# Storing the last 512 columns of the last half row in six transfers of 64, 15, 14, 13, 12 and 10 partitions

## The chip, the core and the metric

The kernel runs on one core of a Trainium2 chip. The core has compute engines that run side by side, each with its own instruction stream: TensorE (PE, unused here), VectorE (DVE), ScalarE (ACT), GpSimd (POOL) and SyncE (SP). Data moves between the chip's memory (HBM) and the on-chip memory (SBUF, 128 partitions) by transfers that an engine issues and that 16 transfer (DMA) engines carry out. Engines wait for each other and for transfers on semaphores.

The metric is the device time of one execution in microseconds (us), median of several runs. Before the change it is 932.68 us (three runs, 932.66 to 932.68). A profiled execution gives the trace; its "span" goes from the start of the program's first instruction to the end of its last one.

## What is computed

The input x is 8192 x 8192 in float32; the output is 8192 x 4096. It is a gated linear unit: the left half of each row times the sigmoid of its right half.

```python
def reference(x: np.ndarray) -> np.ndarray:
    a, b = np.split(x, 2, axis=-1)
    return a * (1 / (1 + np.exp(-b)))
```

The kernel reads 268.44 MB and writes 134.22 MB.

## The kernel before

**Tiles.** The rows go in 32 tiles of 256 rows: each of the 128 partitions holds two rows of x, one behind the other. A tile of x is 128 x 16384 numbers (64 KB in each partition), a tile of the output 128 x 8192 (32 KB in each). There are two input slots (`xs`) and two output slots (`os`), and tile i uses slot i % 2. Positions in a tile are counted in eighths: `(lo, hi)` in `store` are eighths of the output tile, so that `(6, 8)` is the last quarter of it, which is the second half of the second row of each partition, 2048 columns.

**One tile.** SyncE loads it (`load`, L63). ScalarE computes the sigmoid in place over the right halves (`work`, L82). GpSimd multiplies the first 3/16 of the columns and VectorE the rest (L84). ScalarE issues the store (`store`, L68). The first and the last tile are worked in four pieces of 2048 columns, all on VectorE. The first tile is loaded and stored in two halves; the last one is stored as `(0, 4)`, `(4, 6)` and `(6, 8)`, and `behind[-1] = 1` puts the store of a piece behind the sigmoid of the next piece on ScalarE.

**Order and waits.** The order on each engine is that of the program text (`place` keeps it). `place` also drops every wait but those named: a store waits for the multiplies of its piece, a load for the multiplies that last read its slot, the sigmoid for its load and, in the middle tiles, for the store that frees the output slot. The framework gives each transfer, of loads and stores alike, one of eight semaphores in turn. A transfer that takes a semaphore waits on its engine until the one that had it before is over, where the engine doesn't know that already.

**Start and end.** `_launch_early` moves the first load ahead of the start-up barrier. `_close_on_sync` rewrites the end of the program. It finds the semaphore `last` of the last transfer that ScalarE issues in program order (L137). GpSimd waits for the other engines' drains, then for every other transfer and engine (one event for each wait; two waits can share an instruction), drains, clears all semaphores but `last` and drains again; SyncE has one instruction, which waits for `last` and sets it back:

```python
last = [i for i in body if i.engine == ACT and i.opcode == "DMACopy"][-1].sync_info.on_update[0].id
...
    block[:] = [
        *arrive,
        drain1,
        gather1,
        *(event(POOL, w) for w in waits.sync_info.on_wait if w.id != last),
        reset,
        *clears,
        drain2,
        event(SP, final[0], [back]),
    ]
```

In the profile the events and drains of the end stand under L186 (`tc.compile()`), the clears under L152.

Of the kernel before, what the change touches and what calls it, by code (L numbers as in the profile page):

```python
# [8 lines left out]
def _tiles(ctx, tc, x, out):  # L9
    nc = tc.nc  # L10
    P = nc.NUM_PARTITIONS
    DEP = mybir.DependencyInfo(mybir.DependencyClass.Sync, mybir.DependencyReason.DATA)
    fp32 = mybir.dt.float32
    SIG = mybir.ActivationFunctionType.Sigmoid

    n_rows, n_cols = x.shape
    half = n_cols // 2
    R = 2
    SLOTS = 2
    n_tiles = n_rows // (P * R)  # L20
    x_g = x.rearrange("(g p h r) m -> g h p (r m)", p=P, h=2, r=R)
    out_g = out.rearrange("(g p h r) m -> g h p (r m)", p=P, h=2, r=R)

    pool = ctx.enter_context(tc.tile_pool(name="io", bufs=1))
    xs = [pool.tile([P, R * n_cols], fp32, name=f"x_sb{k}") for k in range(SLOTS)]
    os = [pool.tile([P, R * half], fp32, name=f"o_sb{k}") for k in range(SLOTS)]

    whole = [(0, 8)]
    rows = [(0, 4), (4, 8)]
    cut = half // 16 * 3  # L30
    few_and_most = [(0, 8, 0, cut), (0, 8, cut, half)]
    fourths = [(k, k + 2, k % 4 * half // 4, (k % 4 + 2) * half // 4) for k in range(0, 8, 2)]
    loads = [whole] * n_tiles
    works = [few_and_most] * n_tiles
    stores = [whole] * n_tiles
    behind = [0] * n_tiles
    loads[0] = stores[0] = rows
    works[0] = works[-1] = fourths
    stores[-1] = [(0, 4), (4, 6), (6, 8)]
    behind[-1] = 1  # L40

    def meet(a, b):
        return a[0] < b[1] and b[0] < a[1]

    traced = [[] for _ in range(SLOTS)]
    load_of, mul_of, store_of = {}, {}, {}

    def place(i, ins, *needs):


        kept = {n.ins.name for n in needs}
        for e in traced[i % SLOTS]:
            if e.ins.name not in kept:
                tc.declare_no_dep(ins.ins, e.ins, reason="follows from the waits that are kept")
        traced[i % SLOTS].append(ins)
        tc.keep_in_program_order(ins)
        return ins

    def load(i):
        for lo, hi in loads[i]:  # L60
            c = slice(lo * n_cols // 4, hi * n_cols // 4)
            free = [m for w, m in mul_of.get(i - SLOTS, []) if meet(w, (lo, hi))]
            ins = nc.sync.dma_start(out=xs[i % SLOTS][:, c], in_=x_g[i // 2, i % 2, :, c])  # L63
            load_of.setdefault(i, []).append(((lo, hi), place(i, ins, *free)))

    def store(i, lo, hi):
        c = slice(lo * half // 4, hi * half // 4)
        ins = nc.scalar.dma_start(out=out_g[i // 2, i % 2, :, c], in_=os[i % SLOTS][:, c])  # L68
        done = [m for w, m in mul_of[i] if meet(w, (lo, hi))]
        store_of.setdefault(i, []).append(((lo, hi), place(i, ins, *done)))  # L70

    def work(i, lo, hi, near, far):

        rows = xs[i % SLOTS].rearrange("p (r h m) -> p r h m", r=R, h=2)
        packed = os[i % SLOTS].rearrange("p (r m) -> p r m", r=R)
        r, c = slice(lo // 4, (hi + 3) // 4), slice(near, far)
        b = rows[:, r, 1, c]
        landed = [s for w, s in load_of[i] if meet(w, (lo, hi))]
        gone = [s for w, s in store_of.get(i - SLOTS, []) if meet(w, (lo, hi))]
        by_sigmoid = 0 < i < n_tiles - 1  # L80
        needs = [*landed, *(gone if by_sigmoid else ())]
        sig = place(i, nc.scalar.activation(out=b, in_=b, func=SIG), *needs)  # L82
        engine = nc.gpsimd if far == cut and i > 1 else nc.vector
        mul = engine.tensor_mul(out=packed[:, r, c], in0=rows[:, r, 0, c], in1=b)  # L84
        if by_sigmoid:
            for s in gone:
                tc.add_manual_dep(sig.ins, s.ins.name, DEP, reason="frees the output slot")
        place(i, mul, sig, *(() if by_sigmoid else gone))
        mul_of.setdefault(i, []).append(((lo, hi), mul))

    for i in range(SLOTS):
        load(i)
    for i in range(n_tiles):
        due = list(stores[i])
        for k, piece in enumerate(works[i]):
            work(i, *piece)
            ready = works[i][k - behind[i]][1] if k >= behind[i] else 0
            while len(stores[i]) > 1 and k < len(works[i]) - 1 and due[0][1] <= ready:
                store(i, *due.pop(0))
        if i + SLOTS < n_tiles:  # L100
            load(i + SLOTS)
        for lo, hi in due:
            store(i, lo, hi)
# [71 lines left out]
@with_exitstack  # L175
def kernel(
    ctx: ExitStack,
    tc: tile.TileContext,
    x: bass.AP,
    out: bass.AP,  # L180
):
    nc = tc.nc
    with ExitStack() as pools:
        _tiles(pools, tc, x, out)
    tc.close()
    tc.compile()  # L186
    _launch_early(nc)
    _close_on_sync(nc)
# [30 lines left out]
```

## Time and profile before

| what | value |
|---|---|
| median of 3 runs | 932.68 us |
| the profiled execution, its time | 932.5 us |
| its span | 931.1 us |
| read and written | 268.44 MB and 134.22 MB, 432 GB/s over the span |
| VectorE, ScalarE, GpSimd busy | 232.5, 229.8 and 99.9 us |
| last multiply ends (VectorE) | 922.75 us |
| last store is issued (ScalarE) | 922.78 us |
| GpSimd's last instruction ends | 929.32 us |
| SyncE's last instruction ends | 931.12 us |

The compute engines are busy for a quarter of the span or less. The profile's rows name a source line, an engine and an operation; "q" behind an engine (ACTq, POOLq) marks what its sequencer does, such as issuing a transfer or waiting on a semaphore. "us to landing" is the time from the issue of a transfer until its completion semaphore has its last increment. A transfer on 128 partitions gives sixteen such increments, one from each transfer engine, and the trace has the time of each.

### The profile page before, as it was taken

The numbers are of one execution on the slowest core, as the hardware profiler recorded it, in microseconds if no ns is written. First come the engines' busy times: TensorE is split into PE (matmuls) and PEld (weight loads), VectorE is DVE, ScalarE is ACT, GpSimd is POOL, SyncE is SP. The second block draws the span as 40 slices with busy tenths as digits, with TensorE's granted clock in tenths as the row PEclk, the third lists the DMA queues.
The fourth block names the chain that finished last, engine by engine and source line by source line (L and its number), as shares of the span: only waits on it lengthen the run. The fifth ranks groups of instructions, "written<-read, shape, count | busy, mean of one in ns | idle before, by whom it ended". The sixth has DMA issues, their size and how long they took to land.

```text
span 931.1 us, 325 instructions
## 1 busy us (share of the span) xinstructions
DVE 232.5 (25%) x39; ACT 229.8 (25%) x69; POOL 99.9 (11%) x33
## 2 busy tenths in 40 slices
DVE  1133311333113331133320333203332033320233
ACT  2123332033320333203332023320233302333023
POOL 0001111011110111101111011110111101111010
DMA  9999999999999999999999999999999999999998
GB/s 405 450 439 417 428 450 424 455 405 428 450 428 450 407 469 409 428 450 427 452 405 450 428 428 450 424 452 408 428 450 428 450 408 465 411 428 450 427 452 383
DMA packets 9793, 402.67 MB, mean 432 GB/s; under 512 B 1088, under 2 KB 1088, under 8 KB 1088
## 3 DMA queue, kind: packets, MB, share of 16 engines
q1 hardware_dynamic: 4752, 268.44, 66.6%
q10 hardware_dynamic: 5040, 134.22, 33.4%
q14 instruction: 1, 0.01, 0.0%
HBM read 268.44 MB, written 134.22 MB: 432 GB/s over the span
## 4 chain that ended last, share of the span: by engine, by line
DMA 75%; DVE 12%; ACT 12%; issue 0%; ACTq 0%; SPq 0%
DMA out_dram<-o_sb 65%; DVE o_sb L84 12%; ACT x_sb L82 12%; DMA x_sb<-in_x_dram 10%; ACTq L68 0%; SPq L63 0%
## 5 line engine op out<-in xcount | busy, mean ns | idle before, releaser
L84 DVE TENSOR_TENSOR o_sb<-x_sb 128x6656 f32<-128x6656 f32 (+2 forms) x39 | 232.5, 5970 | 690.2 <-ACT x_sb L82 690.2
L82 ACT ACTIVATE x_sb<-x_sb 128x1536 f32<-128x1536 f32 (+1 forms) x68 | 228.5, 3407 | 689.9 <-DMA out_dram<-o_sb 630.0
L84 POOL TENSOR_TENSOR o_sb<-x_sb 128x1536 f32<-128x1536 f32 x29 | 99.7, 3437 | 787.7 <-ACT x_sb L82 787.7
L82 ACT ACT_TABLE_LOAD x1 | 1.3, 1283 | 0.8 <-PEq L203 0.8
L203 POOL MEMSET const-float32-0.0<- 128x1 f32 x1 | 0.1, 98 | 0.2 <-issue 0.2
L203 POOL MEMSET const-bfloat16-1.0<- 128x1 bf16 x1 | 0.1, 101 | 0.0
L203 POOL MEMSET const-uint8-127<- 128x1 uint8 x1 | 0.1, 101 | 0.0
L203 POOL MEMSET const-float32-1.0<- 128x1 f32 x1 | 0.1, 98 | 0.0
## 6 DMA issues: line engine op xcount, KB each, us to landing
out_dram<-o_sb ACTq DMA_DIRECT2D x30, 4096.0 KB, 43.6
x_sb<-in_x_dram SPq DMA_DIRECT2D x2, 4096.0 KB, 16.4
out_dram<-o_sb ACTq DMA_DIRECT2D x3, 2048.0 KB, 28.0
out_dram<-o_sb ACTq DMA_DIRECT2D x2, 1024.0 KB, 8.3
x_sb<-in_x_dram SPq DMA_DIRECT2D x31, 43.5
```

Source lines behind the costliest of these rows:

```text
L82: sig = place(i, nc.scalar.activation(out=b, in_=b, func=SIG), *needs)
L84: mul = engine.tensor_mul(out=packed[:, r, c], in0=rows[:, r, 0, c], in1=b)
L203: nc = _bacc.Bacc("TRN2", target_bir_lowering=False, num_devices=1)
```

## The change

The last store of the last tile, 128 partitions x 2048 columns (8 KB in each partition), becomes seven transfers, issued one behind the other by ScalarE: first 1536 columns of all 128 partitions, then the last 512 columns (2 KB in each partition) of partitions 0 to 63, 64 to 78, 79 to 92, 93 to 105, 106 to 117 and 118 to 127. All of them wait for the same multiply as the one store did. Everything else is as before; the bytes written are the same.

With seven transfers in place of one, the last transfer in program order, whose semaphore is `last` in `_close_on_sync`, is that of partitions 118 to 127. Three of the new transfers wait for an older transfer that had their semaphore: the one of 14 partitions for the store of tile 29, that of 12 for the store of tile 30, that of 10 for the store `(0, 4)` of the last tile.

```diff
+    EDGE = 512
...
     def store(i, lo, hi):
-        c = slice(lo * half // 4, hi * half // 4)
-        ins = nc.scalar.dma_start(out=out_g[i // 2, i % 2, :, c], in_=os[i % SLOTS][:, c])
+        first, end = lo * half // 4, hi * half // 4
+        pieces = [(0, P, first, end)]
+        if (i, hi) == (n_tiles - 1, 8):
+            pieces, p = [(0, P, first, end - EDGE)], 0
+            for n in (64, 15, 14, 13, 12, 10):
+                pieces.append((p, p + n, end - EDGE, end))
+                p += n
+            assert p == P
         done = [m for w, m in mul_of[i] if meet(w, (lo, hi))]
-        store_of.setdefault(i, []).append(((lo, hi), place(i, ins, *done)))
+        for p, q, a, b in pieces:
+            ins = nc.scalar.dma_start(out=out_g[i // 2, i % 2, p:q, a:b], in_=os[i % SLOTS][p:q, a:b])
+            store_of.setdefault(i, []).append(((lo, hi), place(i, ins, *done)))
```

## The prediction, made before the result was known

> **What bounds the kernel now.** I read the page first, then the chain of waits from 897 us on, then the timeline of the last microseconds, and last the rows of the two source lines that close the program.
>
> ```profile
> GB/s 405 450 439 417 428 450 424 455 405 428 450 428 450 407 469 409 428 450 427 452 405 450 428 428 450 424 452 408 428 450 428 450 408 465 411 428 450 427 452 383
> HBM read 268.44 MB, written 134.22 MB: 432 GB/s over the span
> out_dram<-o_sb ACTq DMA_DIRECT2D x2, 1024.0 KB, 8.3
> ```
>
> Transfers run at one rate from the first slice to the last, so the bytes set the time, and the change moves none of them. It can only act on what follows the last multiply. The timeline there:
>
> ```profile
> 918.13 0.34 ACTq L68 DMA_DIRECT2D out_dram<-o_sb  x1
> 920.33 2.79 ACTq L68 DMA_DIRECT2D out_dram<-o_sb  x2
> 920.46 2.29 DVE L84 TENSOR_TENSOR o_sb<-x_sb 128x2048 f32<-128x2048 f32 x1 [0.16 <-ACT x_sb L82]
> ```
>
> The last multiply ends at 922.75 and the last store is issued at 922.78. That row of the page says a 1 MB store lands 8.3 us after its issue: 931.1, the end of the span. Those 8.3 us are a queue, not a latency: by the trace's landing records the last four stores landed at 921.34, 926.20 (2 MB), 928.64 and 931.09 (1 MB each), so 4.86 us for 2 MB and 2.44 for 1 MB. The transfer engines have work without a gap until the end, and an issue is early by several microseconds. Last, the closing instructions, on GpSimd and on SyncE:
>
> ```profile
> L186 POOLq EVENT_SEMAPHORE  x5: 17/43/5235, 923.3 to 928.9; - x5
> L186 POOLq DRAIN  x2: 34/58/83, 929.0 to 929.3; - x2
> L152 POOLq EVENT_SEMAPHORE_RANGE_CLEAR  x2: 66/68/69, 929.1 to 929.2; - x2
> L186 SPq EVENT_SEMAPHORE  x1: 17/17/17, 931.1 to 931.1; - x1
> ```
>
> GpSimd waits for every store but the last one: its wait of 5.235 us (from 923.44) ends at 928.67, 0.03 after the store before the last has landed. Four short waits, a drain, two clears and a drain follow, and it is done at 929.32: **0.68 us after that landing**. SyncE alone waits for the last store, and its one wait is over 0.03 after it. So GpSimd's closing lies beside the 2.44 us of the last store, with 1.8 us to spare.
>
> **The change part by part.** Sums are made against the profiled execution: span 931.1, time 932.5, which is 0.18 under the median of 932.68.
>
> *Issues.* One issue on ScalarE becomes seven. An issue row is 0.34 us with some 0.04 between, so 6 x 0.38 = 2.3 us more on ScalarE, from 923.12 to about 925.4. The semaphores of transfers are used again in turn, eight in all, so three of the new issues also wait for older transfers. The 14-row piece needs the store issued at 868.2 and the 12-row piece the store that landed at 921.34; both are over. The 10-row piece needs the 2 MB store, landed at 926.20, so it goes out at 926.2 to 926.6. Nothing is queued behind it on ScalarE but the drain, for which GpSimd's closing waits at its start, and the last bytes are due only near 930.5. Cost 0; the cover is the queue of bytes. From an issue to a first packet the first load shows about 1.0 us, so an issue could be about 2.5 us later before it costs. SyncE's queue is empty by then and GpSimd issues no transfer.
>
> *Bytes on each engine.* The two sizes give the price of a row. A store of 8 KB rows takes 2.44 us for 8 rows on each of the 16 engines, 0.306 a row; 16 KB rows take 4.86, 0.607. So 8 KB cost 0.3016 and a row itself about 0.004; a 6 KB row is 0.230 and a 2 KB row 0.080. A completion mark is 0.009 in the packet records. Before, each engine has 8 x 0.306. After, it has 8 x 0.230 = 1.84, four rows of the 64-row piece, and, if the five small pieces put one row each on an engine, none to five more. With nine small rows that is 1.84 + 0.72 + 0.05 for five or six more marks = 2.61, or **+0.17 us**; with four it is 2.17, or **-0.27 us**. The 16 marks of the last store land between 930.54 and 931.09: twelve within 930.70, then 930.80, 930.85, 930.90 and 931.09. If the latest engine gets four small rows, it ends at 930.82, and the ordinary ones, with nine, at up to 930.87. If it gets nine it ends at 931.26. The trace does not number its engines, so I take the middle, 931.07, and keep 930.87 and 931.26 as ends.
>
> [...]
>
> *The closing.* This is the step that costs. The last store by program order, for which SyncE waits, is now the 10-row piece. GpSimd waits for all the others, and the 1536-column store and five of the small pieces now end with the whole: no more than one 2 KB row (0.09) before it. The 1.8 us of cover are gone. The six others land at 930.82 to 931.17, in the middle 931.0; 0.68 more makes GpSimd's end 931.68 (ends 931.5 and 931.85), and that is the new end of the span: **+0.56 us** (+0.38 to +0.73).
>
> *Behind the span.* The profiled execution has 1.4 us there. The trace's semaphore records show one semaphore (number 2) counted up at 929.84 and 929.89, then at 931.26 and four more times to 931.42. The first is 0.52 after GpSimd's last instruction, 931.26 is 0.14 after SyncE's. I read this as the engines signing off in turn, SyncE last. If GpSimd is last, its own 0.52 and two steps of 0.05 and 0.04 follow it, 0.61 instead of 0.14: **+0.47 us**. The ends are 0 (the pairing is mine and no view names it) and 0.47; I take 0.47, as it is the nearest record.
>
> Sum: 0.56 + 0.47 = 1.03; 932.5 + 1.03 = 933.53 in the profiled execution, 933.7 for the median.
>
> **The rivals.** All against 0.2% (1.87 us: 930.81 and 934.55), about what a measurement of this kernel can tell from no change.
>
> *A, the closing stays hidden or the balance pays.* The late engine gets four small rows (-0.22), nothing is added behind the span, and the 10-row piece lands well after the others, since it is issued over 1 us after them. For it: late marks keep their offsets over the last ten stores (+0.44, +0.26, +0.21, +0.16), so they belong to fixed engines. Against it: with bytes queued until 930.5 the late issue changes no order. Time: 932.68 - 0.22 = 932.5, up to 932.8 if half of GpSimd's 0.68 shows.
>
> *B, neighbouring rows share a way out of memory.* Every transfer of this trace spans all 128 partitions, and 432 GB/s over 16 engines is what those give; a piece of 15 neighbouring rows has no row here. One end is 0. [...] As the pieces before the last end 0.22 earlier, 933.7 + 1.4 - 0.2 = 934.9; with two pieces overlapping, about 934.2. From 0.84 us on it makes the change slower by over 0.2%.
> [...] I take the nearest row, full rate, and keep this as the upper end.
>
> *C, the small pieces pile up (the other side: slower).* 15, 14, 13, 12 and 10 rows don't divide over 16 engines. If a piece lies on one engine or a few, one engine gets up to 64 rows at 0.080 instead of five: +4.7 us, 938.4. It decides from 16 rows on one engine: 11 more than five at 0.080 are 0.9 us. Against it: all records of 128-row stores show 16 marks, the rows shared out.
>
> **How the numbers follow.** The forecast (closing laid bare, rows at full rate, 932.9 to 934.3) has 0.62; A 0.15 (932.4 to 932.8); B 0.18 (933.9 to 935.0, some 0.07 of it above 934.55); C 0.05. No mechanism takes 1.87 us off: 0.01 for faster, from A. Slower is 0.07 + 0.05 = 0.12, the rest, 0.87, is within 0.2%. The range goes from A's 932.4 to B's 934.9.
>
> **What would show it.** GpSimd's last drain should end after SyncE's last wait, near 931.7, as the end of the span; its long wait should end near 931.0, not 928.67. ScalarE should show eight issues after 920 us, the last at 926.2. The last landing should be 930.9 to 931.3; 932 and later speaks for B, 934 and later for C. If GpSimd ends before SyncE, the step on the closing was wrong. If its end is last but the time behind the span stays at 1.4 us, the 0.47 was.

## The result and the profile after

The changed kernel takes **934.65 us** (median of 15 runs, 934.47 to 934.80) against 932.68 us before (15 runs, 932.60 to 933.04): +1.97 us, a ratio of 1.0021 with a 95% interval of 1.0013 to 1.0029. The forecast was 933.7 with a range to 934.9, so the direction and about half of the size were there. The interval is clear of 1, but it leaves open on which side of the forecast's mark of 0.2% the change lies. The profiled execution shown here has a time of 934.65 and a span of 932.8.

The bytes and their rate are the same. The lines of the page that answer to those of before, with the last store now in seven parts (of each row of issues: the number, the size of one transfer and its time from issue to landing, where the page has one):

```profile
HBM read 268.44 MB, written 134.22 MB: 432 GB/s over the span
out_dram<-o_sb ACTq DMA_DIRECT2D x1, 1024.0 KB, 8.3
out_dram<-o_sb ACTq DMA_DIRECT2D x1, 768.0 KB, 8.2
out_dram<-o_sb ACTq DMA_DIRECT2D x1, 128.0 KB, 8.1
out_dram<-o_sb ACTq DMA_DIRECT2D x1, 30.0 KB, 7.0
```

The wide part is a quarter smaller than the store that it came from, yet it lands 8.2 us after its issue instead of 8.3. By the forecast's prices of a row, 8 x 0.306 before and 8 x 0.230 now, it should have saved some 0.6 us. That is the first thing to explain.

The timeline of the last microseconds, and ScalarE's issue rows (duration in ns: least, median, most):

```profile
920.61 10.10 ACTq L78 DMA_DIRECT2D out_dram<-o_sb  x8
920.74 2.29 DVE L93 TENSOR_TENSOR o_sb<-x_sb 128x2048 f32<-128x2048 f32 x1 [0.16 <-ACT x_sb L91]
```
```profile
L78 ACTq DMA_DIRECT2D out_dram<-o_sb x7: 338/1221/1653, 923.1 to 930.4; - x7
```

Seven issues take from 923.06 to 930.70, not to 926.6. The first and the last take 0.34, those between take 0.98 to 1.65. That is the second thing to explain.

The closing, by its source lines (number of instructions, duration in ns, start of the first and the last):

```profile
L195 POOLq EVENT_SEMAPHORE  x5: 17/43/354, 931.0 to 932.4; - x5
L195 POOLq DRAIN  x2: 34/58/83, 932.4 to 932.7; - x2
L195 SPq EVENT_SEMAPHORE  x1: 17/17/17, 932.5 to 932.5; - x1
L161 POOLq EVENT_SEMAPHORE_RANGE_CLEAR  x2: 48/68/88, 932.5 to 932.6; - x2
```

SyncE's wait for the last store is over at 932.485; GpSimd still drains and clears until 932.775, and that is now the end of the span. Before it was the other way round, with 1.8 us between them.

The last mark of each transfer, from the trace's landing records, in us. I take these for the marks of one transfer engine, the latest: before the change the last mark of each of the last ten stores came 0.42 to 0.46 us behind the middle of its sixteen. One column is one transfer; the last row is the distance from the mark before:

```
                 1 MB     1536 columns   64     15     14     13     12     10
before  928.64   931.09
after   928.89   931.23                  931.57 931.75 931.93 932.10 932.28 932.45
step             2.35                    0.34   0.18   0.18   0.17   0.18   0.17
```

The execution after is 0.25 us behind from earlier on (928.89 against 928.64). Measured from there, the last mark came 2.44 us later before and 3.56 us later now: **the landing is 1.1 us later**. Two places hold it. The 1536 columns take 2.35 instead of the 1.84 that their rows cost, 0.5 too much; and the five small pieces take 0.176 each where a row and a mark were to cost 0.089.

Behind the span the order of the signing off shows as forecast: semaphore 2 goes up 0.52 after GpSimd's last instruction, at 933.30, then at 933.34 and 933.37. The time at which it reached SyncE's step was 931.26 before: 2.11 later, or 1.86 without the 0.25.

### The profile page after: what moved, and what is told of

Same layout as the page of the kernel before. It is cut to its first block, busy times and chain, and to the rows that moved or that the text cites. A ratio compares the mean times of both kernels' runs of the same rounds, so it can differ in the third digit from the quotient of the medians.

```text
span 932.8 us, 331 instructions
## 1 busy us (share of the span) xinstructions
DVE 232.5 (25%) x39; ACT 229.8 (25%) x69; POOL 99.8 (11%) x33
## 4 chain that ended last, share of the span: by engine, by line
DMA 75%; DVE 12%; ACT 12%; issue 0%; ACTq 0%; SPq 0%
DMA out_dram<-o_sb 65%; DVE o_sb L93 12%; ACT x_sb L91 12%; DMA x_sb<-in_x_dram 10%; ACTq L78 0%; SPq L64 0%
```

## The experiments

Three theories stood at the start, and the expectations add a fourth. **Closing**: 0.75 us of the loss is GpSimd's closing laid bare. **Sharing**: the rest comes from transfers of few or neighbouring partitions, which keep each other from the full rate. **Issues**: the rest comes from ScalarE's slow issues, which let the transfer engines run dry. **Price of a transfer**: each further one costs some 0.2 us, whatever its shape. All times below are medians of ten runs beside runs of the kernel before on the same chip (932.66, 932.61 and 932.64 us in the three groups), unless it is said that there was one. The 95% intervals of the ratios reach about 0.1% to each side, and those of e4 (0.9996 to 1.0015) and e5 (0.9998 to 1.0016) hold 1; there the single runs and the marks in the traces have to carry the reading.

### The closing alone

e1 is the kernel before with the two waits of the closing exchanged:

```diff
-    last = [i for i in body if i.engine == ACT and i.opcode == "DMACopy"][-1].sync_info.on_update[0].id
+    last = [i for i in body if i.engine == ACT and i.opcode == "DMACopy"][-2].sync_info.on_update[0].id
```

> The kernel before, with one store per piece as it was; only the closing is exchanged: SyncE waits for the store before the last, GpSimd for the last one. Theory 'closing laid bare': GpSimd is done 0.68 us after the last landing (931.1 + 0.7 = 931.8) and signs off 0.6 later, so +1.1 us: 933.8. Rival 'the closing is not on the path': 932.7.

Measured: 933.76, +1.10 us (ratio 1.0010, 1.0000 to 1.0019). No transfer has changed. The closing rows of e1:

```profile
L186 POOLq EVENT_SEMAPHORE  x5: 17/43/7671, 923.7 to 931.7; - x5
L186 POOLq DRAIN  x2: 34/58/83, 931.8 to 932.0; - x2
L186 SPq EVENT_SEMAPHORE  x1: 17/17/17, 929.0 to 929.0; - x1
```

GpSimd's long wait (from 923.78, 7.671 us) ends at 931.45 with the last landing, its last drain at 932.08; semaphore 2 goes up 0.52 after that. A closing that starts when the last transfer lands costs this kernel 1.1 us.

e2 is the changed kernel with the closing mended: SyncE waits for all seven transfers of the last store, and GpSimd neither waits for their semaphores nor clears them.

```diff
-    last = [i for i in body if i.engine == ACT and i.opcode == "DMACopy"][-1].sync_info.on_update[0].id
-    final = [w for w in waits.sync_info.on_wait if w.id == last]
+    copies = [i for i in body if i.engine in (ACT,) and i.opcode == "DMACopy"][-7:]
+    late = sorted({c.sync_info.on_update[0].id for c in copies})
+    final = [w for c in copies for w in waits.sync_info.on_wait if w.id == c.sync_info.on_update[0].id]
...
-        *(event(POOL, w) for w in waits.sync_info.on_wait if w.id != last),
+        *(event(POOL, w) for w in waits.sync_info.on_wait if w.id not in late),
...
-        event(SP, final[0], [back]),
+        *(event(SP, w, [b]) for w, b in zip(final, back)),
```

> The changed kernel, but SyncE waits for all seven transfers of the last store and GpSimd only for what is older, so that its clears lie beside the last transfers again. In the trace of the changed kernel SyncE's sign-off would come at 932.62 instead of 933.37, so theory 'the closing costs 0.75 of the loss' expects 933.9; the rest, 1.2 us, is the later landing. If the closing costs nothing: 934.65.

Measured: 933.85, 0.80 less than the changed kernel. Its closing rows:

```profile
L200 SPq EVENT_SEMAPHORE  x7: 17/17/17, 931.3 to 932.6; - x7
L200 POOLq DRAIN  x2: 34/58/83, 931.3 to 931.5; - x2
```

GpSimd is done at 931.55, while SyncE's seven waits follow the marks of the latest engine, from 931.34 to 932.58. So of the 1.97 us the closing holds 0.8, and 1.2 are the later landing. All the kernels below but e8 and e10 have the mended closing (for as many transfers as they have in the last store), so that they show the landing alone.

### Full and half transfers

e3 and e4 store the last 512 columns in one transfer of 128 partitions, and in two of 64:

```diff
-            pieces, p = [(0, P, first, end - EDGE)], 0
-            for n in (64, 15, 14, 13, 12, 10):
...
+            pieces = [(0, P, first, end - EDGE), (0, P, end - EDGE, end)]   # e3
+            for n in (64, 64):                                              # e4
```

> The last 512 columns in one transfer of all 128 partitions behind the one of 1536 columns, closing mended as in e2 (SyncE waits for both). Theory 'sharing' (only rows of neighbouring partitions without the other half cost): 932.7, one mark and eight short rows more, 0.05. Theory 'issues' (ScalarE's slow issues set the end): 932.7 too, one issue more is far from late. Theory 'price of a transfer' (every further transfer costs 0.2 or so whatever its shape): 932.9.

Measured: 932.70, +0.04: no difference. One more full transfer was as good as free here.

> The last 512 columns in two transfers of 64 partitions each, closing mended. [...] Theory 'issues': two issues of 1.3 us end by 926.2, nothing late: 932.7. Theory 'price of a transfer': 932.9 to 933.0.

Measured: 933.38, +0.72. Issues and price of a transfer had put it at 932.7 and at 933.0 at most. With a wide row held up by 0.5 as in the changed kernel (728 ns instead of 234) the 932.70 of e3 becomes 933.2, so of the theories sharing is left. e12 then changes only which partitions are in a half, the even and the odd ones instead of the lower and the upper:

```diff
+            pieces = [(0, P, first, end - EDGE)]
+            pieces += [(slice(k, P, 2), None, end - EDGE, end) for k in range(2)]
```

> As e4 (1536 columns, then two transfers of 64 partitions, closing mended), but the two take every second partition, the even and the odd ones, instead of the lower and the upper half. [...] If 64 rows in a transfer cost by themselves: 933.4 as e4.

Measured: 932.73, +0.09 us. The same number of transfers, rows and issues as e4, and the loss is gone: the ten runs of e4 took 933.17 to 933.49, those of e12 932.65 to 932.89. The transfers issued after the last multiply, in e4 and in e12 (size of one, time from issue to landing):

```profile
out_dram<-o_sb ACTq DMA_DIRECT2D x1, 768.0 KB, 8.3
out_dram<-o_sb ACTq DMA_DIRECT2D x2, 128.0 KB, 7.8
```
```profile
out_dram<-o_sb ACTq DMA_DIRECT2D x1, 768.0 KB, 7.7
out_dram<-o_sb ACTq DMA_DIRECT2D x2, 128.0 KB, 7.2
```

It is the wide transfer *ahead* of the half one that lands 0.6 us later in e4. The packet records say how: in e3 and e12 all 128 rows of 6 KB take 234 ns; in e4 one takes 791 ns, in the changed kernel one takes 728, in e2 764, in e6 638, in e7 720. In e2, e4, e6 and e7 the next longest 6 KB row takes at most 248 ns; in e11, below, four take 295 to 846. The latest engine is still at its last wide row when the others have begun with partitions 0 to 63 (in the changed kernel from 930.18 on, the first of the others at 929.76), and by these records that row goes at about a third of its rate (728 against 234). Rows of the half transfer suffer too: a 2 KB row takes up to 346 ns in e4 and never over 84 in e12. In e10, below, 64 partitions come directly behind the 1 MB store, and there it is an 8 KB row of that store that takes 747 ns instead of 309. So it is shown that the choice of partitions makes the loss, and with it the 0.5 us on the wide part. On which side the sharing lies is not: with the partitions the runs also changed which rows of the output in HBM are written at the same time. In this choice of partitions and of output rows alone e4 and e12 differ, by 0.65 us.

### The small pieces

e6 makes the small pieces even, four times 16 neighbouring partitions; e7 takes every fourth partition for each of the four instead.

```diff
+            for n in (64, 16, 16, 16, 16):                                                       # e6
...
+            pieces = [(0, P, first, end - EDGE), (0, 64, end - EDGE, end)]                       # e7
+            pieces += [(slice(64 + k, P, 4), None, end - EDGE, end) for k in range(4)]
```

> After the 1536 columns 64 partitions and then four times 16 neighbouring ones, closing mended: one row on each engine, even. Theory 'sharing': as e2 with four one-row pieces instead of five, at the 0.18 that their marks lie apart on the latest engine: 933.7. Theory 'uneven pieces' (a piece that doesn't fill 16 engines is what costs): 933.4, as e4, or less.

Measured: 933.62, 0.23 under e2, or 0.18 when each is taken against its own runs of the kernel before. Sixteen rows in each piece are no cure; one piece less saved about its 0.18.

> As e6, but each piece of 16 takes every fourth partition of 64 to 127 instead of 16 neighbours. [...] If the 0.18 is the price of a row with its mark whatever its partition, as e6: 933.7.

Measured: 933.64, as e6 (933.62): in the time the choice of the partitions makes no difference here. The marks of the latest engine are 0.18 apart in both (e6: 931.46, 931.64, 931.81, 931.99, 932.16; e7: 931.44, 931.62, 931.80, 931.97, 932.15). For the latest engine it did not matter which neighbours a piece has; in both runs 0.18 was the price of a transfer that puts one row on an engine.

In the packet records the neighbours did matter. From 930.8 on, when the last piece of 16 is under way, ten rows of 2 KB take 101 to 265 ns in e6; in e7 none takes over 88. In the changed kernel five rows at 931.2 take 113 to 161. But these rows lie on engines that are done before the latest one, whose small rows take 84 ns in both kernels, so the time does not show them.

e11, with one run, has pieces that halve:

```diff
-            for n in (64, 15, 14, 13, 12, 10):
+            for n in (64, 32, 16, 8, 4, 2, 2):
```

> After the 1536 columns pieces of 64, 32, 16, 8, 4, 2 and 2 partitions, closing mended. A look at the marks: the latest engine's mark should go on in steps of 0.18 as long as it takes part. [...] Time with sharing: 933.5 to 934.2.

Measured: 934.21, at the upper edge. The latest engine's marks come at 931.25 (the wide one), 931.60 (64), 931.78 (32), 931.96 (16), 932.13 (8), 932.31 (4), 932.48 (2) and 932.65 (2). Each transfer has one: the latest engine took part even in those of two rows. And 32 partitions, two rows on an engine, cost the same 0.18 as one row, while four rows cost 0.34. So two marks of this engine stood no closer than about 0.175, and two rows of 2 KB with their mark (2 x 0.080 + 0.009 = 0.17) just fill that time.

In the changed kernel the landing records of the transfers of 15, 14, 13, 12 and 10 partitions show as many marks, from 930.70 on, and one record more for each, 0.09 to 0.17 us after its issue ends (926.48, 927.58, 928.84, 930.50 and 930.88). The latest engine's mark is there in each, so it got nine small rows, not four.

### The issues

e5 cuts the last store into seven transfers of all 128 partitions, 288 or 296 columns each:

```diff
+            at = [first + n * (end - first) // 7 // 8 * 8 for n in range(7)] + [end]
+            pieces = [(0, P, a, b) for a, b in zip(at, at[1:])]
```

> The last store in seven transfers as in the changed kernel, but each of all 128 partitions (288 or 296 columns), closing mended. Theory 'sharing': nothing shares a way, so only rows and marks: 48 rows and 6 marks more on each engine at 0.004 and 0.009, some 0.25 us, 932.9. Theory 'issues': the issues are as slow as in the changed kernel (about 1.3 us each, the last one done near 930.7), each brings only 0.35 us of bytes, so the engines run dry and the last lands near 932: 933.7. Theory 'price of a transfer' (0.18 for each further one instead of 0.09): 933.2.

Measured: 933.28, +0.67. The issue rows of e5:

```profile
L75 ACTq DMA_DIRECT2D out_dram<-o_sb x7: 338/1184/1277, 923.1 to 929.3; - x7
```

Five of them are about as slow as in the changed kernel (the last two take 0.65 and 0.46), with no small and no uneven piece, so it is not the shape that makes an issue slow. But the marks of the latest engine come 0.42 to 0.44 us apart without a hole (929.39, 929.83, 930.26, 930.70, 931.13, 931.57, then 931.96), so the latest engine did not wait for the issues, and the 933.7 of that theory was missed. The time came out where "price of a transfer" had put it, yet the rows explain most of it: a row of 1152 or 1184 bytes takes 51 or 52 ns in the packet records, not 46. Seven transfers of eight such rows and a mark are 7 x (8 x 0.0515 + 0.009) = 2.95 us against 2.48 for the one store in the same records: 0.47 of the 0.54 by which the last mark came later. My row price, fitted to rows of 8 and 16 KB, was too low for short ones.

e9 has SyncE issue the six pieces:

```diff
-            ins = nc.scalar.dma_start(out=out_g[i // 2, i % 2, p:q, a:b], in_=os[i % SLOTS][p:q, a:b])
+            engine = nc.sync if b - a == EDGE else nc.scalar
+            ins = engine.dma_start(out=out_g[i // 2, i % 2, p:q, a:b], in_=os[i % SLOTS][p:q, a:b])
```

> The changed kernel with the closing mended as in e2, but SyncE issues the six pieces, in a queue of its own, while ScalarE issues the 1536 columns. Theory 'issues': SyncE's issues take 0.34 each, all out by 925.5, so the time falls to 932.9. Theory 'latest engine' (the held-up wide row and 0.18 for each piece on the latest engine): the same work is on that engine, only in another order: 933.3 to 933.9.

Measured: 934.14, above both expectations. The issue rows:

```profile
L79 SPq DMA_DIRECT2D out_dram<-o_sb x6: 547/1267/1619, 923.0 to 929.5; - x6
L79 ACTq DMA_DIRECT2D out_dram<-o_sb x1: 338/338/338, 923.0 to 923.0; - x1
```

SyncE's queue holds nothing older (its last load landed at 912.0), and its issues are as slow. The two queues also mix: the wide transfer lands at 931.76, 0.4 later than in e2, and 6 KB rows of up to 447 ns show that more of them are held up. An issue that is slow because of its own engine's queue is out.

e8, with one run, has the same pieces cut from the first store of the program:

```diff
-        if (i, hi) == (n_tiles - 1, 8):
+        if (i, hi) == (0, 4):
```

> A look at the issue rows: the same six pieces cut from the first store of the program, when ScalarE's queue holds nothing older; the closing is as before the change. Theory 'backlog' (an issue is held while ScalarE's older transfers are queued): 0.34 us each. Theory 'behind another' (an issue directly behind another one takes 1.0 to 1.6 whatever is queued): 1.0 to 1.6 again. Time 932.7 to 934.

```profile
L78 ACTq DMA_DIRECT2D out_dram<-o_sb x7: 292/387/823, 18.4 to 21.6; - x7
```

Neither theory: 0.29 to 0.82, with 0.53 and 0.82 for the second and the third and 0.29 to 0.39 for the others. So an issue directly behind another isn't slow by itself. What makes it slow at the end of the program was not settled. The time of e8, 935.17, points to a cause of its own: six more transfers shift the turn of the eight semaphores, and SyncE's load of tile 2 now has that of the load of tile 1, which is in flight until 45.7. The load of tile 2 lands at 72.90 instead of 70.46, and the span is 2.7 us longer; the delay was not tried by itself. The timelines from 18 us on, before and in e8:

```profile
28.15 0.33 SPq L63 DMA_DIRECT2D x_sb<-in_x_dram  x1
```
```profile
45.83 0.33 SPq L64 DMA_DIRECT2D x_sb<-in_x_dram  x1
```

e10 puts the six pieces ahead of the wide transfer, with the closing as the change left it:

```diff
             assert p == P
+            pieces = pieces[1:] + pieces[:1]
```

> The changed kernel with its own closing, but the six pieces are issued before the 1536 columns, so that the last transfer is a wide one of 1.84 us and covers GpSimd's 0.68 again. If the slow issues (1.0 to 1.6 each) put the wide store's issue near 930, the engines run dry before it and it lands near 933: 934.5 to 935. If they don't matter: the 0.75 of the closing is saved and the pieces cost their 0.62 or less: 933.0 to 933.8.

Measured: 933.36, where the second expectation put it, though not for its reason. The issue rows:

```profile
L79 ACTq DMA_DIRECT2D out_dram<-o_sb x7: 340/532/1655, 922.9 to 928.7; - x7
```

The last transfer is a wide one again, so GpSimd is done at 930.92, beside it. But its 16 marks lie within 0.24 us (931.75 to 931.99), where in the other kernels with a wide part at the end they are spread over 0.6 to 1.3: all engines began it together, that is, they had run dry and waited for its issue at 928.67. By the packet records 5 of the 16 engines were at work on the mean from 928.6 to 929.5. Here the slow issues do set the end, and the time stayed low because the last three issues were short again (0.39, 0.34 and 0.36). In the changed kernel the issues come close to setting the end, no more: from 930.6 to 931.6 some 5 of the 16 engines are at work, the others wait for pieces, but the latest one has its steps of 0.18 to the end.

## Why the prediction was right or wrong

Right, by its own steps:

- **The closing is laid bare.** GpSimd ends after SyncE and ends the span. e1 has it alone at +1.10, the sum of the forecast's 0.68 and 0.47 less the few hundredths that SyncE's own wait took; e2 finds 0.80 of it in the changed kernel. It is less there because GpSimd waits for the semaphores one after another: before, three more waits followed the one that ended with the landing; behind the landing of the 12-row piece (932.28) only one more does, so 0.50 instead of 0.68 followed. (The forecast counted four short waits behind the long one; its row has three, as the first of the five is the wait for the drains. The 0.68 was read from the ends and stands.)
- **The sign-off behind the span.** 0.52 after GpSimd's end and 0.07 to SyncE's step, as read from the semaphore records before.
- **Rivals A and C.** The closing did not stay hidden, the latest engine did not get four rows, and the 10-row piece landed 0.17 behind the piece before it, so A is out. Each small piece has as many marks as rows, so nothing piled up on one engine, and C is out.

Left open by the forecast: **which end of the bytes.** The latest engine got nine small rows. The forecast kept that end and took the middle, 0.19 less.

Wrong:

- **"Bytes on each engine".** The term that failed: the last mark was put at 931.07, its bad end at 931.26; it came at 932.20 (932.45 less the 0.25 by which this execution was behind). Against the bad end 0.94 us are missing: 0.5 is the latest engine's last 6 KB row, held up by the 64-partition piece (e4 against e12), and 0.43 are five steps of 0.176 instead of 0.089. A row of 2 KB was rightly 0.08 and a mark rightly 0.009 in the packet records, but two marks of the latest engine came no closer than 0.173 (e6, e7, e11).
- **Rival B** came to 934.9 with 1.4 us for the sharing and 0.22 taken off for pieces that end earlier. No run shows either term. In their place the runs showed 0.5 that the 64-row piece cost on the wide row of the engine that was late anyway, and 0.43 for the five steps. Rows of the pieces themselves are held up too (up to 265 ns in a piece of 16 in e6, up to 346 in a piece of 64 in e4), but on engines that end early.
- **"Issues", cost 0.** The cost was nearly right, the size was not: 0.34 each was taken from issues that stand alone, and those in the middle took 0.98 to 1.65. Its cover, put at 2.5 us, was used up by a delay of 4.1; e10 shows what a little more would have cost.

The sum: 1.03 us were forecast. The marks that GpSimd waits for came 1.03 later than put (932.28 less 0.25, against 931.0), and its closing was 0.18 shorter: 1.88, about as in the trace (1.86). The medians differ by 1.97; the last 0.1 is not placed.

That the result lies inside the stated range is in part luck. The forecast's own band ended at 934.3; the range reaches 934.9 only through rival B, by terms that no run shows. By the forecast's own sign (a last landing of 932 and later speaks for B) the trace spoke for B. A time above 934.55, such as this one, had a chance of only 0.12.

No version here beats the kernel before: e3 (+0.04) and e12 (+0.09) are as fast, the others came out slower.

## What to carry to other kernels

When the last transfer is split, look first at what runs beside it: here a closing of 0.68 us and a sign-off of 0.47 were hidden by one long last transfer, and a split whose pieces end together laid them bare, as GpSimd waits for all transfers but one. A price per row that was fitted to large transfers did not hold for a transfer with one row on an engine (steps of 0.176 us in place of 0.089). A row that was held up cost time here only on the engine that ended last: the times of e6 and e7 are 933.62 and 933.64, their longest small rows from 930.8 on 265 and 88 ns. And a transfer over a part of the partitions is to be judged by what it does to the one ahead of it: here it slowed the engine that was late by 0.5 us and doubled its lag behind the middle of the marks, from 0.41 at the store before to 0.91.

## What the runs showed of the hardware that was not expected

- Two marks of the latest transfer engine came no closer than about 0.175 us in the runs with one queue, whether one or two rows of 2 KB lay between them. The packet records do not show this: in the changed kernel the last rows start 0.086 apart, and the last packet ends at 931.67, 0.79 before the last mark; before the change that distance was 0.31. What holds the marks was not tried.
- Most issues one behind the other took 0.98 to 1.66 us in the last microseconds, on ScalarE and on SyncE alike and also for 128 partitions (1.26 in e3), but 0.29 to 0.82 near the start, and in some kernels the last ones were short again (0.34 in the changed kernel, 0.34 to 0.39 in e10). The cause is open.
- A few transfers more near the start of the program delayed a load by 17.7 us through the turn of the eight semaphores (e8).
- Sixteen neighbouring partitions with one row on each engine slowed rows of 2 KB to as much as 265 ns, where every fourth partition left them at 88 or less (e6, e7).
